# Four-entry projections: the second token tile unit by unit, and a ninth buffer for split weights

## The chip, the cores and the metric

The kernel runs on one core of a Trainium2 chip. The metric is the device time of one execution in microseconds; of several runs the median is taken. Durations inside an execution come from one profiled run, which records every instruction of the five engines: TensorE (PE, matmuls), VectorE (DVE), ScalarE (ACT), GpSimd (POOL) and SyncE (SP, which issues the loads).

## The reference

A transformer of two blocks on 256 tokens of 1024 features, in fp32. What matters here, cut down:

```python
def first_block(x, p, ...):
    h = h + 0.5 * _swiglu(_rmsnorm(h, ffn1_norm), ffn1_w_in, ffn1_w_out)      # f1
    z = _rmsnorm(h, mix_norm) @ w_in                                          # mi
    h = h + concatenate([_conv_module(...), _gla(...)]) @ w_out               # mo
    h = h + 0.5 * _swiglu(_rmsnorm(h, ffn2_norm), ffn2_w_in, ffn2_w_out)      # f2
    gate = sigmoid(_rmsnorm(h, ple_norm) @ ple_w_gate)                        # pg
    h = h + gate * (p @ ple_w_proj)                                           # pp
    return _rmsnorm(h, final_norm)

def second_block(x, c, ...):
    for i in range(2):
        mod = silu(c) @ ada_w[i] + ada_b[i]                                   # ada
        x = x + 0.5 * g1 * swiglu(modulate(rms_norm(x, ...), sh1, sc1), ...)  # f3, f5
        h = modulate(rms_norm(x, ...), sh2, sc2)
        mix = diff_attention(h, ...) if i == 0 else spatial_gating(h, ...)    # qkv, wo; si, so
        x = x + g2 * mix
        x = x + 0.5 * g3 * swiglu(modulate(rms_norm(x, ...), sh3, sc3), ...)  # f4, f6
        x = rms_norm(x, ln_out[i])
    return x
```

The comments are the names that the kernel gives to the weights of each stage. The SwiGLU's inner width is 2816.

## The kernel before, in words

**Tokens and weights.** The 256 tokens are two tiles of 128 (`NT`). All weights come from HBM as a stream of 317 tiles of 1 MB, in the order in which the stages use them; the tile with number i is called `raw`i while it is loaded. `N_RAW = 3` tiles are in flight or in use at a time, so a load is issued when the tile three before it is done with. A tile is two units of 128 x 1024.

**Split weights.** To keep fp32 accuracy, each unit is split in a high half `wh`, an ACT cast (L208), and a low half `wl`, a DVE subtraction (L209). Activations are split in the same way (`xh` and `xl`, `g`, `yHL`, `cHL`, `oHL`; L513 and L514). Every product is three matmuls: high by high, high by low, low by high (L505 to L507, and L707 where the weights are stationary). `N_HL = 8` is the number of units that may be live as pairs `wh`, `wl`; `wh14_0` is the high half of unit 0 of tile 14. Tiles of kind `ada` are not split: DVE multiplies them by `cact` and accumulates (L462).

**What sets the order.** `Stream.pump` walks the stream and issues the next cast and subtraction as soon as fewer than `N_HL` units are live. `get` hands a unit to a matmul; `release` says that its last matmul has been issued, and pumps. The program is written once, in Python, and each instruction is given a priority; every engine then runs its instructions in the order that results. So the number of live units and the place of a release decide where a cast stands among ACT's other work.

**The FFNs.** An FFN works in 11 chunks of 256 inner columns (`NCH`). From the third chunk on, `chunkT` computes gate and up of a chunk for both token tiles at once (L707, tile `gu`, two banks of 128 columns each); `evac` takes SiLU of the gate on ACT (`s`, L749), multiplies by up on DVE (`g`, L751), and splits `g`. The down products go to `acc`, four banks of 128 x 512 (two token tiles by two column halves), and are issued between the gate/up matmuls of later chunks. The banks of `gu` are used in turn: the next chunk's first matmul needs the `g` that last read its bank. In f1, ACT also makes scaled identity matrices for the convolution (`diag`, L853).

**The four-entry projections.** `pg`, `wo` and `so` (1024 x 1024) are four weight tiles, eight units, worked by `down2`: token tile 0, first four units; token tile 1, units 0 and 1; tile 0, last four units, after which `fin(0)` adds tile 0 to the residual `h0` and starts its norm; then token tile 1, the six units left, first column half and then second; `fin(1)`. `down` releases a unit in the second column half. The norm that follows is, for each tile t, a sum of squares on ACT (`ss`), `nv`t on DVE (L533), an rsqrt on POOL (`rn`, L519), `xn` on DVE and ACT (L575, L577), a transpose on PE (`xT`, L586), the modulation `xa` on DVE and ACT (L595, L599), and the split `xh`, `xl` (L513, L514).

Of the kernel before, what the change touches and what calls it, by code (L numbers as in the profile page):

```python
# [21 lines left out]
NT = S // P  # L22
# [8 lines left out]


N_RAW = 3
N_HL = 8
BUFS = {
    "row": (4, 4), "b4": (6, 4),
    "c0": (3, 2), "c1": (3, 2), "g2": (8, 2), "m": (6, 2), "ev": (4, 1),
# [118 lines left out]
def w_at(key):  # L156

    stationary = (key[0].endswith("_gu") and key[1] >= HEAD) or key[:2] in (("mi", 1), ("mi", 2))
    return W_AT if stationary else 0


class Stream:
# [23 lines left out]
    def pump(self, now=False, n=0):  # L186
# [4 lines left out]
        while 2 * self.n_split + self.half < end and (now or not k.held):  # L191
# [3 lines left out]
            if key[0] == "ada":  # L195
# [3 lines left out]
                continue  # L199
            if len(self.live) >= N_HL:  # L200
                return
            u = self.half
            raw = self.raw[i]
            at = slice(w_at(key), w_at(key) + 1024)
            h = k.wpool.tile([P, 1024 + W_PAD], F32R, tag="wh", name=f"wh{i}_{u}", bufs=N_HL)[:, at]
            l = k.wpool.tile([P, 1024 + W_PAD], F32R, tag="wl", name=f"wl{i}_{u}", bufs=N_HL)[:, at]
            with k.ahead(-BEHIND):
# [29 lines left out]
class Kernel:  # L237
# [423 lines left out]
    def fin(self, **kw):  # L661
        def f(t):
            self.xtask[t] = self.spawn(self.finish(t, **kw))
        return f
# [37 lines left out]
    def mmT(self, out, w, x, first, last):  # L702
# [6 lines left out]
            )  # L709
        self.tick(0.33)  # L710

    def down(self, t, units, first, last):

        for hf in range(2):
            sl = slice(hf * 512, hf * 512 + 512)
            for n, (key, u, x) in enumerate(units):
                h, l = self.ws.get(key, u)
                self.mm3(
                    self.acc[t][hf], x, (h[:, sl], l[:, sl]), first and n == 0, last and n == len(units) - 1
                )  # L720
                if t == NT - 1 and hf == 1:
                    self.ws.release(key, u)

    def down2(self, name, order, xs, fin):


        self.new_acc()

        def units(t, g, lo=0, hi=4):
            x = xs(t, g)  # L730
            e = order[2 * g : 2 * g + 2]
            return [((name, e[n // 2]), n % 2, x[n]) for n in range(lo, hi)]

        self.down(0, units(0, 0), True, False)
        self.down(1, units(1, 0, 0, 2), True, False)
        self.down(0, units(0, 1), False, True)
        fin(0)
        self.down(1, units(1, 0, 2, 4) + units(1, 1), False, True)
        fin(1)

    def ffn(self, name, fin):
# [944 lines left out]
```

## Time and profile before

| | |
|---|---|
| median of three runs | 1484.52 us |
| the three runs | 1482.23, 1484.52, 1487.17 us |
| the profiled run | 1483.39 us |
| its span, first to last instruction | 1481.6 us |
| PE / DVE / ACT busy | 98% / 73% / 53% of the span |
| granted TensorE clock, mean | 0.999 |
| HBM read | 343.47 MB, 233 GB/s over the span |
| 16 DMA engines busy, main queue | 62.8% |

The span of the profiled run is 1.8 us short of its time, and the profiled run is 1.1 us short of the median. "Busy" is the time in which an engine had an instruction under way. Matmuls are pipelined, so a matmul's own duration is longer than the time from its start to the start of the next; where PE's pace matters, the starts are read. A note such as [0.36 <-DVE xn] behind a row says that the engine was idle for 0.36 us before it and that the DVE instruction that wrote `xn` ended the wait.

### The profile page before, as it was taken

Reading aid. Unit: us, or ns where it says so; the run is one execution under the profiler, and the core shown is the slowest. Engines: PE = TensorE matmul, PEld = TensorE weight load, DVE = VectorE, ACT = ScalarE, POOL = GpSimd, SP = SyncE. Lnnn points to the kernel's source line nnn. Section 1 sums busy time; section 2 is a strip of 40 time slices with the busy share of each in tenths; the row PEclk is TensorE's granted clock in tenths of the full one; section 3 lists DMA queues with packets and bytes.
Section 4 is the critical chain, followed back from the end, with each engine's and each line's share of the span. In section 5 each row is a group of like instructions: output and inputs, shape, how many; then the busy total and the mean of one; then the engine's idle time right before and its main releaser. Section 6 shows DMA issues by size and latency. Waiting matters only on the chain.

```text
span 1481.6 us, 23272 instructions
## 1 busy us (share of the span) xinstructions
PE 1456.1 (98%) x9256; PEld 1299.3 (88%) x9256; DVE 1084.9 (73%) x1694; ACT 781.1 (53%) x1238; POOL 51.2 (3%) x59
## 2 busy tenths in 40 slices
PE   8999999999999999999999999999999999999997
PEld 6999989779999878999777899998899988899997
DVE  6876569978765687875688888866887668685554
ACT  6554566265444684444587544446544455554442
POOL 1000000100000000000021100000000000000000
PEclk9999999999999999999999999999999999999999
DMA  8887545138776448786345389963898846376550
GB/s 320 337 309 272 188 150 182 67 127 319 302 274 247 160 148 318 303 322 230 141 162 198 142 330 347 345 228 125 324 341 347 289 150 229 111 289 226 207 206 29
DMA packets 52333, 346.06 MB, mean 234 GB/s; under 512 B 5913, under 2 KB 8705, under 8 KB 11777
## 3 DMA queue, kind: packets, MB, share of 16 engines
q1 hardware_dynamic: 52224, 344.58, 62.8%
q8 instruction: 72, 1.18, 0.3%
q14 instruction: 37, 0.30, 0.1%
HBM read 343.47 MB, written 1.09 MB: 233 GB/s over the span
## 4 chain that ended last, share of the span: by engine, by line
PE 82%; DVE 9%; ACT 3%; issue 2%; DMA 2%; POOL 2%; SPq 0%; POOLq 0%; DVEq 0%; ACTq 0%
PE gu L707 40%; PE acc L506 9%; PE acc L507 9%; PE acc L505 9%; DVE wl L209 4%; PE gu L506 2%; PE gu L505 2%; PE gu L507 2%; DMA raw<-wpack 2%; PE xT L586 1%; ACT wh L208 1%; DVE cacc L839 1%; POOL rn L519 1%; PE cv L863 1%; PE qkv L505 0%
## 5 line engine op out<-in xcount | busy, mean ns | idle before, releaser
L209 DVE TENSOR_TENSOR wl<-raw,wh 128x1024 fp32r<-128x1024 f32 x490 | 588.4, 1221 | 242.4 <-ACT wh L208 240.2
L208 ACT CAST wh<-raw 128x1024 fp32r<-128x1024 f32 x490 | 502.4, 1051 | 397.3 <-DMA raw<-wpack 166.9
L707 PE MATMUL gu<-xh,wh 128*128 128x256 f32 x1728 | 484.3, 280 | 1.2 <-DVE g L751 0.8
L707 PE MATMUL gu<-xl,wh 128*128 128x256 f32 x1728 | 482.5, 279 | 0.0
L707 PE MATMUL gu<-xh,wl 128*128 128x256 f32 x1728 | 482.0, 279 | 0.0
L707 PEld LDWEIGHTS gu<-xh,wh 128*128 128x128 f32 x1728 | 324.8, 188 | 4.6 <-DVE g L751 1.4
L707 PEld LDWEIGHTS gu<-xl,wh 128*128 128x128 f32 x1728 | 324.8, 188 | 2.5
L707 PEld LDWEIGHTS gu<-xh,wl 128*128 128x128 f32 x1728 | 324.8, 188 | 0.0
L506 PE MATMUL acc<-wh,g 128*128 128x512 f32 x528 | 206.7, 391 | 0.0
L507 PE MATMUL acc<-wl,g 128*128 128x512 f32 x528 | 206.1, 390 | 0.0
L505 PE MATMUL acc<-wh,g 128*128 128x512 f32 x528 | 205.7, 391 | 0.0
L462 DVE SCALAR_TENSOR_TENSOR raw<-raw,cact 128x1024 f32<-128x1024 f32 x144 | 171.7, 1218 | 16.4 <-DMA raw<-wpack 16.3
L507 PEld LDWEIGHTS acc<-wl,g 128*128 128x128 f32 x528 | 99.1, 188 | 21.0
L506 PEld LDWEIGHTS acc<-wh,g 128*128 128x128 f32 x528 | 99.1, 188 | 19.8 <-DVE g L514 1.4
L505 PEld LDWEIGHTS acc<-wh,g 128*128 128x128 f32 x528 | 99.1, 188 | 19.2
L749 ACT ACTIVATE s<-gu 128x256 f32<-128x256 f32 x108 | 40.8, 385 | 76.2 <-PE gu L707 76.0
L505 PE MATMUL gu<-wh,xh 128*128 128x512 f32 x192 | 75.7, 395 | 2.0 <-ACT wh L208 1.6
L507 PE MATMUL gu<-wl,xh 128*128 128x512 f32 x192 | 75.1, 393 | 1.5 <-DVE wl L209 1.5
L506 PE MATMUL gu<-wh,xl 128*128 128x512 f32 x192 | 75.2, 393 | 0.5 <-DVE xl L514 0.5
L751 DVE TENSOR_TENSOR g<-gu,s 128x256 f32<-128x256 f32 x108 | 44.5, 420 | 28.2 <-ACT s L749 28.1
L513 ACT CAST g<-g 128x256 fp32r<-128x256 f32 x108 | 43.1, 405 | 39.1 <-DVE g L751 38.4
L519 POOL TENSOR_TENSOR rn<-nv,neghalf 128x1 f32<-128x1 f32 (+1 forms) x22 | 20.1, 913 | 1238.1 <-DVE nv L533 1020.6
(308 smaller groups left out, 1611.3 us busy)
## 6 DMA issues: line engine op xcount, KB each, us to landing
raw<-wpack SPq DMA_DIRECT2D x316, 1024.0 KB, 5.0
gate<-grow SPq DMA_DIRECT2D x6, 512.0 KB, 4.6
row<-rows SPq DMA_DIRECT2D x5, 512.0 KB, 5.7
bias<-fd SPq DMA_DIRECT2D x16, 128.0 KB, 3.9
raw<-wpack SPq DMA_DIRECT2D x2, 512.0 KB, 6.7
out<-h SPq DMA_DIRECT2D x4, 256.0 KB, 2.2
h<-x SPq DMA_DIRECT2D x2, 256.0 KB
h<-x SPq DMA_DIRECT2D x1, 512.0 KB
```

The source lines that it names most:

```text
L208: self.last = k.after(nc.scalar.copy(out=h, in_=raw[:, u, :]))
L209: self.last_l = k.after(nc.vector.tensor_sub(out=l, in0=raw[:, u, :], in1=h.bitcast(F32)))
L462: self.after(nc.vector.scalar_tensor_tensor(out=raw[:, u, :], in0=raw[:, u, :], scalar=1.0, in1=self.cact, op0=ALU.mult, op1=ALU.mult, acc ...
L505: nc.tensor.matmul(out, lhsT=xh, rhs=wh, start=first, stop=False)
L506: nc.tensor.matmul(out, lhsT=xl, rhs=wh, start=False, stop=False)
L507: nc.tensor.matmul(out, lhsT=xh, rhs=wl, start=False, stop=last)
L513: self.nc.scalar.copy(out=dst[0], in_=src),
L519: self.nc.gpsimd.tensor_tensor(out=r, in0=v, in1=self.neghalf[:, :n], op=ALU.pow)
L586: self.last_T = nc.tensor.transpose(ps[:, i, :], xn[hf][:, i * P : (i + 1) * P], self.ident)
L707: nc.tensor.matmul(out, lhsT=ww, rhs=xx, start=first and n == 0, stop=last and n == 2, skip_group_check=True)
L749: nc.scalar.activation(s, b[:, 0, :], AF.Silu)
L751: nc.vector.tensor_mul(out=y, in0=b[:, 1, :], in1=s)
```

## The change

`N_HL` goes from 8 to 9. In `down2` the last call for token tile 1 is taken apart: the two units that are left of the first four go through the new `down_by_unit`, which does both column halves of a unit and releases it at once; the last four units go through `down` as before.

```diff
-N_HL = 8
+N_HL = 9
...
+    def down_by_unit(self, units):
+
+
+        for key, u, x in units:
+            h, l = self.ws.get(key, u)
+            for hf in range(2):
+                sl = slice(hf * 512, hf * 512 + 512)
+                self.mm3(self.acc[NT - 1][hf], x, (h[:, sl], l[:, sl]), False, False)
+            self.ws.release(key, u)
+
...
         fin(0)
-        self.down(1, units(1, 0, 2, 4) + units(1, 1), False, True)
+        self.down_by_unit(units(1, 0, 2, 4))
+        self.down(1, units(1, 1), False, True)
         fin(1)
```

Behind the new function the lines of the file are 10 or 11 higher: SiLU in an FFN is L749 before and L760 after, the SwiGLU product L751 and L762, the convolution's `diag` L853 and L864.

How the order of the engines' instructions moves is shown at three places. The names carry the tile's name and a running number; the rows stand in program order.

**First place: ACT and DVE in f1, third chunk.** ACT before, from the cast of weights 12 on; `s_75` and `s_78` are the SiLUs of the third chunk's two banks `gu_51` and `gu_52`:

```order
L208 CAST wh12_0_524<-raw12_402 128x1024
L208 CAST wh12_1_573<-raw12_402 128x1024
L853 ACTIVATE diag_72_560<-kc_80,cols_81 128x128
L749 ACTIVATE s_75_583<-gu_51_416 128x256
L749 ACTIVATE s_78_588<-gu_52_417 128x256
L513 CAST g_77_587<-g_76_585 128x256
L208 CAST wh14_0_619<-raw14_498 128x1024
L513 CAST wglr_64_542<-wg_63_540 128x8x16
L513 CAST g_80_592<-g_79_590 128x256
L208 CAST wh14_1_626<-raw14_498 128x1024
L208 CAST wh15_0_658<-raw15_577 128x1024
```

ACT after, from the same cast:

```order
L208 CAST wh12_0_500<-raw12_396 128x1024
L208 CAST wh12_1_528<-raw12_396 128x1024
L208 CAST wh14_0_583<-raw14_474 128x1024
L864 ACTIVATE diag_73_570<-kc_80,cols_81 128x128
L208 CAST wh14_1_623<-raw14_474 128x1024
L208 CAST wh15_0_632<-raw15_532 128x1024
L208 CAST wh15_1_662<-raw15_532 128x1024
L760 ACTIVATE s_75_587<-gu_51_420 128x256
L864 ACTIVATE diag_73_570<-kc_80,cols_81 128x128
L760 ACTIVATE s_78_592<-gu_52_421 128x256
```

The two SiLUs stood ahead of all four casts of weights 14 and 15; now the first stands behind the four, and the second behind one more `diag`. DVE in the same place, before, from the last subtraction of weights 12; `g_76` and `g_79` are the SwiGLU products made from `s_75` and `s_78`:

```order
L209 TENSOR_TENSOR wl12_1_574<-raw12_402,wh12_1_573 128x1024
L462 SCALAR_TENSOR_TENSOR raw13_406,ada_31_252<-raw13_406,cact_88 128x1024 x2
L751 TENSOR_TENSOR g_76_585<-gu_51_416,s_75_583 128x256
L478 TENSOR_TENSOR mod_86_713<-ada_31_252,cols_81 128x8
L751 TENSOR_TENSOR g_79_590<-gu_52_417,s_78_588 128x256
L481 SCALAR_TENSOR_TENSOR mod_86_713<-mod_86_713,cols_81 128x8
L514 TENSOR_TENSOR g_77_587<-g_76_585,g_77_587 128x256
L209 TENSOR_TENSOR wl14_0_620<-raw14_498,wh14_0_619 128x1024
```

DVE after:

```order
L209 TENSOR_TENSOR wl12_1_529<-raw12_396,wh12_1_528 128x1024
L462 SCALAR_TENSOR_TENSOR raw13_400,ada_31_252<-raw13_400,cact_88 128x1024 x2
L478 TENSOR_TENSOR mod_86_689<-ada_31_252,cols_81 128x8
L481 SCALAR_TENSOR_TENSOR mod_86_689<-mod_86_689,cols_81 128x8
L209 TENSOR_TENSOR wl14_0_584<-raw14_474,wh14_0_583 128x1024
L209 TENSOR_TENSOR wl14_1_624<-raw14_474,wh14_1_623 128x1024
L209 TENSOR_TENSOR wl15_0_633<-raw15_532,wh15_0_632 128x1024
L209 TENSOR_TENSOR wl15_1_663<-raw15_532,wh15_1_662 128x1024
L762 TENSOR_TENSOR g_76_589<-gu_51_420,s_75_587 128x256
L462 SCALAR_TENSOR_TENSOR raw16_536,ada_84_668<-raw16_536,cact_88 128x1024
```

The product `g_76` stood right behind the `ada` step on tile 13, ahead of the subtractions of weights 14; now it stands behind those of weights 14 and 15, and `g_79` behind the first step on the `ada` tile 16.

**Second place: PE in f1, where the gate/up matmuls of the next chunk begin.** They write the bank `gu_82` and use weights 9; `acc_47` to `acc_50` are the four banks of the down product. Before:

```order
L507 MATMUL acc_47_412<-wl12_1_574,g_61_451 128x512
L505 MATMUL acc_48_413<-wh12_0_524,g_59_445 128x512
L506 MATMUL acc_48_413<-wh12_0_524,g_59_445 128x512
L507 MATMUL acc_48_413<-wl12_0_525,g_59_445 128x512
L707 MATMUL gu_82_632<-xh_86,wh9_0_388 128x256
L707 MATMUL gu_82_632<-xl_87,wh9_0_388 128x256
L707 MATMUL gu_82_632<-xh_86,wl9_0_389 128x256
L707 MATMUL gu_82_632<-xh_86,wh9_0_388 128x256
```

After:

```order
L506 MATMUL acc_50_419<-wh12_0_500,g_59_449 128x512
L507 MATMUL acc_50_419<-wl12_0_501,g_59_449 128x512
L505 MATMUL acc_50_419<-wh12_1_528,g_61_455 128x512
L506 MATMUL acc_50_419<-wh12_1_528,g_61_455 128x512
L507 MATMUL acc_50_419<-wl12_1_529,g_61_455 128x512
L707 MATMUL gu_82_636<-xh_86,wh9_0_382 128x256
L707 MATMUL gu_82_636<-xl_87,wh9_0_382 128x256
L707 MATMUL gu_82_636<-xh_86,wl9_0_383 128x256
L707 MATMUL gu_82_636<-xh_86,wh9_0_382 128x256
```

Before, nine down matmuls of weights 12 stand ahead of the first gate/up matmul and the other fifteen behind the chunk; now all twenty-four stand ahead, up to the last on `acc_50`.

**Third place: DVE at the start of f4, the norm of token tile 1 after `wo`.** `gy` and `h1` are the residual's second column half, `nv1` and `xn` the norm. Before:

```order
L552 TENSOR_TENSOR gy_1075_8572<-acc_1019_8315,gate_686_6464 128x512
L209 TENSOR_TENSOR wl171_0_8516<-raw171_8287,wh171_0_8515 128x1024
L554 TENSOR_TENSOR h1_79<-gy_1075_8572,h1_79 128x512
L209 TENSOR_TENSOR wl171_1_8520<-raw171_8287,wh171_1_8519 128x1024
L533 SCALAR_TENSOR_TENSOR nv1_1078_8580<-ss1_1068_8556 128x1
L209 TENSOR_TENSOR wl172_0_8526<-raw172_8309,wh172_0_8525 128x1024
L575 TENSOR_SCALAR xn_1081_8590<-h1_79,rn1_1079_8582 128x512
L209 TENSOR_TENSOR wl172_1_8530<-raw172_8309,wh172_1_8529 128x1024
```

After, to the same `xn`:

```order
L209 TENSOR_TENSOR wl171_1_8520<-raw171_8281,wh171_1_8519 128x1024
L552 TENSOR_TENSOR gy_1075_8576<-acc_1019_8319,gate_686_6462 128x512
L209 TENSOR_TENSOR wl172_0_8526<-raw172_8303,wh172_0_8525 128x1024
L554 TENSOR_TENSOR h1_79<-gy_1075_8576,h1_79 128x512
L209 TENSOR_TENSOR wl172_1_8530<-raw172_8303,wh172_1_8529 128x1024
L209 TENSOR_TENSOR wl173_0_8536<-raw173_8413,wh173_0_8535 128x1024
L533 SCALAR_TENSOR_TENSOR nv1_1078_8584<-ss1_1068_8560 128x1
L209 TENSOR_TENSOR wl173_1_8543<-raw173_8413,wh173_1_8542 128x1024
L575 TENSOR_SCALAR xn_1081_8594<-h1_79,rn1_1079_8586 128x512
```

Two subtractions of weights 171 stood ahead of `nv1` and one of 172 ahead of `xn`; now the first unit of 171 is far ahead, and the subtractions go up to `wl173_0` ahead of `nv1` and to `wl173_1` ahead of `xn`. The same shift, with its own numbers, stands in the program at the start of f6, and on DVE at the start of f3 (`wl112_0` instead of `wl111_0` ahead of `xn` of tile 1).

## Rows read from the trace of the kernel before

**Rows 1.** Page, part 1: engine, busy us (share of the span), instructions
```profile
PE 1456.1 (98%) x9256; PEld 1299.3 (88%) x9256; DVE 1084.9 (73%) x1694; ACT 781.1 (53%) x1238; POOL 51.2 (3%) x59
```

**Rows 2.** Waits of PE: instruction and what ended it, us in total, times, longest
```profile
PE xT L586 <- DVE xn L575: 4.6, 11, 0.7
...
PE gu L507 <- DVE wl L209: 1.5, 2, 1.0
...
PE qT L1247 <- DVE qn L1243: 1.3, 1, 1.3
...
PE acc L505 <- ACT cHL L513: 1.1, 1, 1.1
...
PE gu L707 <- DVE g L751: 0.8, 1, 0.8
...
PE gu L707 <- DVE g L790: 0.4, 1, 0.4
```

**Rows 3.** Page, part 5: busy us, mean ns | idle before, releaser
```profile
L209 DVE TENSOR_TENSOR wl<-raw,wh 128x1024 fp32r<-128x1024 f32 x490 | 588.4, 1221 | 242.4 <-ACT wh L208 240.2
...
L208 ACT CAST wh<-raw 128x1024 fp32r<-128x1024 f32 x490 | 502.4, 1051 | 397.3 <-DMA raw<-wpack 166.9
```

**Rows 4.** Timeline of ACT, f1: start us, us, [idle before]
```profile
49.89 2.00 ACT L208 CAST wh<-raw 128x1024 fp32r<-128x1024 f32 x2 [1.70 <-DMA raw<-wpack]
...
52.10 0.64 ACT L749 ACTIVATE s<-gu 128x256 f32<-128x256 f32 x2
...
56.31 1.05 ACT L208 CAST wh<-raw 128x1024 fp32r<-128x1024 f32 x1
```

**Rows 5.** Timeline of DVE, same stretch
```profile
55.54 0.42 DVE L751 TENSOR_TENSOR g<-gu,s 128x256 f32<-128x256 f32 x1
...
56.07 0.42 DVE L751 TENSOR_TENSOR g<-gu,s 128x256 f32<-128x256 f32 x1
```

**Rows 6.** Timeline of PE, same stretch
```profile
55.46 0.39 PE L506 MATMUL acc<-wh,g 128*128 128x512 f32 x1
55.69 0.39 PE L507 MATMUL acc<-wl,g 128*128 128x512 f32 x1
56.02 0.39 PE L707 MATMUL gu<-xh,wh 128*128 128x256 f32 x1
56.24 0.28 PE L707 MATMUL gu<-xl,wh 128*128 128x256 f32 x1
56.36 0.28 PE L707 MATMUL gu<-xh,wl 128*128 128x256 f32 x1
```

**Rows 7.** DMA issues from 53.3 to 53.5: KB each, us to landing
```profile
raw<-wpack SPq DMA_DIRECT2D x1, 1024.0 KB, 5.2
```

**Rows 8.** Timeline of PE, end of the mixer
```profile
304.87 0.50 PE L505 MATMUL acc<-wh,cHL 128*128 128x512 f32 x1 [1.08 <-ACT cHL L513]
```

**Rows 9.** Timeline of DVE, end of the mixer
```profile
304.85 0.69 DVE L514 TENSOR_TENSOR cHL<-cs,cHL 128x512 fp32r<-128x512 f32 x1 [0.22 <-ACT cHL L513]
```

**Rows 10.** Timeline of DVE, start of f3
```profile
542.23 0.49 DVE L575 TENSOR_SCALAR xn<-h,rn 128x512 f32<-128x512 f32 x1 [0.59 <-POOL rn L519]
```

**Rows 11.** Timeline of DVE, attention
```profile
802.96 0.17 DVE L1295 RECIPROCAL rs<-sm 128x4 f32<-128x4 f32 x1
```

**Rows 12.** Timeline of PE, attention
```profile
810.01 0.66 PE L1311 MATMUL aT<-kc,s 128*128 128x128 f32 x4 [0.32 <-DVE on L1348]
```

**Rows 13.** Timeline of DVE, start of f4
```profile
846.14 0.48 DVE L575 TENSOR_SCALAR xn<-h,rn 128x512 f32<-128x512 f32 x1 [0.45 <-POOL rn L519]
```

**Rows 14.** Timeline of PE, start of f4
```profile
846.69 0.65 PE L586 MATMUL xT<-kc,xn 128*128 128x128 f32 x4 [0.36 <-DVE xn L575]
```

**Rows 15.** Timeline of DVE, start of f6
```profile
1294.15 0.49 DVE L575 TENSOR_SCALAR xn<-h,rn 128x512 f32<-128x512 f32 x1 [0.44 <-POOL rn L519]
```

**Rows 16.** Timeline of PE, warming matmuls at the start
```profile
1.50 4.64 PE L436 MATMUL warm<-one,ones_r 128*128 128x512 f32 x10 [1.50 <-POOL one L431]
...
7.73 2.11 PE L436 MATMUL warm<-one,ones_r 128*128 128x512 f32 x8
```

## The prediction

> **What bounds the kernel now.** The page's first part comes first: TensorE (PE) is busy for 1456.1 us of a span of 1481.6, 98% [rows 1]. So the time is PE's matmuls plus the places where PE stands still, and a change that leaves the matmuls alone can only add to or take from the still places. The list of PE's waits says how much there is to take: the largest single kinds are 4.6 us for `xn`, 1.5 for a low half `wl` of the weights, 1.1 for `cHL` and 0.8 for a SwiGLU product `g` [rows 2]. Nothing that a ninth weight buffer could fill is larger than those 1.5 us. Then the page's costliest groups: a unit of weights costs ACT one cast of 1.05 us and DVE one subtraction of 1.22 us, 490 times each [rows 3]. These two are the coins in which this change pays, because in the trace ACT and DVE start their instructions in the order of the program, and the change moves casts and subtractions ahead of other work.
>
> **What the change does.** It adds and removes no matmul, cast, subtraction or load; each engine has as many rows as before. In the four-entry projections the second token tile's first units are freed earlier, and one more unit may be in flight, so nearly every cast and subtraction moves one unit forward. Where the engine in question has only casts around it, that costs nothing. It costs where something that PE waits for stands right behind.
>
> **Step 1, the third chunk of f1.** Before, ACT casts chunk weights 12, then runs SiLU `s_75`, `s_78` at 52.10 and only then casts `wh14_0` at 56.31 [rows 4]. DVE makes the two `g` at 55.54 and 56.07, 0.42 each [rows 5]. PE leaves the `acc` matmuls of weights 12 after the one at 55.69 and starts the next gate/up matmul at 56.02, as soon as the first `g` has freed its PSUM bank: a hole of 0.1 us [rows 6]. After, `s_75` stands behind four more casts, the last two of weights 15; `g` stands behind `wl15_1`; and PE runs 15 more `acc` matmuls before it comes to the gate/up matmul (the order rows show all three).
>
> Fifteen matmuls at the 0.23 us from one start to the next [rows 6] end the cover at 55.92 + 3.45 = 59.37. The load of weights 15 can't start sooner than before: it takes the buffer that `wl12_1` frees, and it was issued at 53.36 and took 5.2 us [rows 7], so it lands at 58.55. Two casts then end at 60.6, `s_75` at 60.9; the two subtractions behind the casts end near 61.95 (the second can't start before 60.6, and the first fills 59.6 to 60.8), and `g_76` at 62.35. PE is idle from 59.37 to 62.4: **3.05 us**. The gate/up matmuls of the chunk's second 128 columns stand seven behind (0.12 us apart [rows 6], so 63.2) and need `g_79`, behind one `ada` multiply-add over a tile of a subtraction's size (1.2, [rows 3]) and a small subtraction (0.1): 62.35 + 1.3 + 0.42 = 64.05, another **0.85**. With 0.2 for the fourth chunk, which is shuffled too but has 17 matmuls of its first 128 columns to run before it needs the second `g`, step 1 is **+4.1**. Low bound 2.6 (load half a microsecond faster, second `g` covered half); high bound 5.8 (fourth chunk not covered: a cast and a `g` more).
>
> **Step 2, end of the mixer.** PE stands 1.08 us for `cHL` before 304.87 [rows 8]. After, ACT has two casts of weights 60 ahead of the activations that make it, where it had the two of weights 59; DVE has three subtractions left before the low half of `cHL` where it had two, which moves that from 304.85 [rows 9] by one, 1.15 less the 0.22 it was idle. **+0.9**, bounds 0 and 1.2.
>
> **Step 3, gate projection to f3.** Here the change helps first: `wl110_0` is made well before the norm, so the longest wait for `wl`, 1.0 us [rows 2], goes. But tile 1's norm chain on DVE gets three subtractions ahead of it instead of one and a `g` inside it, which moves `xn` from 542.23 [rows 10] by about 4 us. PE has tile 0's matmuls of weights 112 moved ahead to cover most; by my row-by-row reckoning tile 1 starts 1.4 us later on balance, and PE reaches the two later waits for `g`, 0.8 and 0.4 us [rows 2], with these done. **0**, bounds -2.7 (the three waits go, 1.0 + 0.8 + 0.4 and the 0.2 or so that a restart costs each; tile 1 hidden) and +1.5.
>
> **Step 4, attention.** `wl168_0` now stands ahead of the softmax reciprocal of 802.96 [rows 11]; its cast waits for two units of ACT work, so the reciprocal moves to about 806.8. Of these 3.9 us PE covers most with value matmuls that it now does first; it already waited 0.32 at the transposes of 810.01 [rows 12], so anything uncovered shows. Between 0, all covered, and 3.9, nothing covered, I choose a third, **+1.2**, since there are value matmuls for the greater part but the transposes wait already.
>
> **Step 5, attention output to f4, gating output to f6.** DVE had `wl171_1` before `nv1`, `wl172_0` before `xn` of tile 1 (846.14 [rows 13]); after, it has `wl172_1`, `wl173_0` before `nv1` and `wl173_1` before `xn` as well. `h1` now ends near 844.1 and is followed by 2.3 us of subtractions, `nv1` at 846.5, another subtraction, `xn` at 847.9 to 848.4: about 1.8 us late. PE waited for it 0.36 us before 846.69 already [rows 14]. Tile 0's matmuls on weights 172 and 173, which come ready sooner, fill 0.9 of this; the low half `xl` behind one more subtraction adds 0.4. **+1.3** each. The gating output has the same rows at 1294.15 [rows 15]: together **+2.6**, bounds 0 and 5.2. Other stage borders (f1 to mixer, f4 to f5) shift by the same one unit on every engine: 0.
>
> **Sum.** 4.1 + 0.9 + 0 + 1.2 + 2.6 = **+8.8 us**. The profiled execution took 1483.39 us (span 1481.6); that makes 1492.2. The median of the runs shown is 1.1 above the profiled one, so a median is forecast at **1493**. The low bounds add to -0.1, the high ones to +17.6.
>
> **A page against the row.** The trace's longest hole in PE inside the kernel is some 1.3 us [rows 2], and the granted clock is 0.999 of 2.4 GHz over the span; a hole of 3.05 us is beyond what it shows. At the start, ten warming matmuls took 4.64 us and eight later ones 2.11, so 0.46 against 0.26 each [rows 16]. If such a slow stretch came after the hole in step 1, it would cost 4.64 - 10 x 0.26 = 2.0 us more. The Trainium skill, "TensorE: Matmul & The Clock Gate", section "Why this matters for your kernels", warns that idle gaps between bursts of matmuls send the array back to half clock; no row here shows it, and by that rule the sum would be 10.8 instead of 8.8. The Trainium skill, "Perfetto Trace Analysis", section "Optimization Strategy", says that the same gap repeating on the engine that should be saturated can mean too few buffers; by it the ninth buffer would gain. PE's waits for `wl` are two in the whole span [rows 2], so the repeating gap isn't there.
>
> **Rivals.**
> *The ninth buffer pays.* The waits of step 3 go (-2.7), and the fillers that the new order moves ahead cover what steps 2, 4 and 5 delay. This needs step 1 to be no loss: the load of weights 15 would have to land by 55.5, 2.1 us after its issue, so that `g` is done by 59.3. The one load took 5.2 us [rows 7]; against. Time 1484.5 - 2.7 = 1481.8, and 1479.5 if half of the 4.6 us that PE waits for `xn` [rows 2] went with it. Chance 0.15.
> *Only f1 loses.* Step 1 stands, step 3 gains its 2.7, and half of steps 2, 4 and 5 is covered (2.35): 4.1 - 2.7 + 2.35 = +3.75, 1488.3, which can't be told from no change. For it: PE has fillers moved ahead at each of these places. Against: PE already waited at each. Chance 0.22, from 1482 to 1488.9.
> *The slow stretch.* Forecast plus 2.0: 1495. Chance 0.06.
> *The forecast*, chance 0.57.
>
> **How the numbers follow.** A measurement of this kernel tells 0.3%, 4.5 us, from no change: faster is under 1480.0, slower over 1489.0. The first rival's two times lie on either side of the lower bound, so its chance is halved between them. Slower: 0.57 + 0.06 = 0.63. Same: 0.22 + 0.08 = 0.30. Faster: 0.07. The range leaves out the faster half of the first rival and the top of the summed bounds, about one in ten at each end: 1481 to 1499; the forecast's own range is 1489 to 1498.
>
> **What would show it.** In the trace after: a hole of about 3 us in PE between 59 and 63, ended by the SiLU product, with `s` starting after the second cast of weights 15; a second hole of nearly 1 us right behind; no wait for `wl` near 537; `xn` of tile 1 about 4 us later near 546, and 1.8 later (after subtracting what PE has lost so far) near 848 and 1296; the reciprocal 4 us later in the attention. The prediction is wrong if PE has no hole near 60, which would say that ACT or the load had more slack than the rows show; or if the holes are there and the time isn't, which would say that PE makes idle time up later, where in this trace there is hardly any to make up.

## The result, and the profile after

The changed kernel takes 1495.15 us in the median (1494.33 to 1495.58, four runs), the kernel before 1483.74 (1482.23 to 1487.17, four runs): a ratio of 1.0073 with a 95% interval of 1.0061 to 1.0085, 0.7% slower. Its profiled run took 1495.58 us, with a span of 1493.4, against 1481.6 before. PE has as many matmuls as before, 9256, and all of the loss lies in the places where it stands still or runs slowly.

Where in the kernel the time goes is read from the first transposes (`xT`) of each stage's norm, which are the same instructions in both traces:

| first `xT` after | before, us | after, us | difference | in this part |
|---|---|---|---|---|
| start | 6.88 | 7.30 | +0.42 | +0.42 |
| f1 | 194.49 | 200.14 | +5.65 | +5.23 |
| mixer | 314.80 | 323.96 | +9.16 | +3.51 |
| f2, gate projection, f3 | 720.61 | 727.72 | +7.11 | -2.05 |
| attention | 835.73 | 845.18 | +9.45 | +2.34 |
| attention output, f4 | 1022.62 | 1033.09 | +10.47 | +1.02 |
| f5 and gating unit | 1283.74 | 1294.42 | +10.68 | +0.21 |
| gating output, f6 (last matmul) | 1473.71 | 1485.57 | +11.85 | +1.17 |

The waits of PE after, in the form of [rows 2] (instruction and what ended the wait, us in total, times, longest):

```profile
PE xT L586 <- DVE xn L575: 4.8, 11, 1.2
PE gu L707 <- DVE g L762: 3.3, 2, 2.7
PE qT L1258 <- DVE qn L1254: 2.0, 2, 1.4
PE gu L506 <- DVE xl L514: 1.9, 4, 0.7
...
PE acc L505 <- ACT cHL L513: 1.4, 1, 1.4
PE gu L507 <- DVE wl L209: 0.8, 2, 0.5
PE acc L506 <- DVE cHL L514: 0.7, 1, 0.7
```

The `g` of L751 is L762 here. Its 3.3 us in two waits are new and lie in f1; the one wait of 0.8 that it had before, in f3, is gone, and so is the wait of 0.4 for the other `g`. `cHL` has grown from 1.1 to 1.4 and its low half has a wait of its own, 0.7; a second wait for `qn` is new; the long wait for `wl` is down from 1.0 to 0.5. The waits for `xl` add up to 1.9 in four; before there was one, in the mixer:

```profile
PE gu L506 <- DVE xl L514: 0.5, 1, 0.5
```

The first hole, in the timeline of PE in f1, where [rows 6] showed 0.1 us:

```profile
59.49 0.39 PE L507 MATMUL acc<-wl,g 128*128 128x512 f32 x1
62.55 0.39 PE L707 MATMUL gu<-xh,wh 128*128 128x256 f32 x1 [2.66 <-DVE g L762]
...
63.36 0.28 PE L707 MATMUL gu<-xh,wh 128*128 128x256 f32 x1
64.32 0.55 PE L707 MATMUL gu<-xh,wh 128*128 128x256 f32 x1 [0.68 <-DVE g L762]
64.67 0.42 PE L707 MATMUL gu<-xl,wh 128*128 128x256 f32 x1
64.89 0.42 PE L707 MATMUL gu<-xh,wl 128*128 128x256 f32 x1
...
67.42 0.28 PE L707 MATMUL gu<-xh,wh 128*128 128x256 f32 x1
67.53 0.28 PE L707 MATMUL gu<-xl,wh 128*128 128x256 f32 x1
```

PE ends the down product with the matmul at 59.49 and starts gate and up at 62.55, 2.83 us after its next slot at 59.72. Behind seven of these matmuls it stands again for 0.68 us. The timeline of ACT shows why; the two casts are those of weights 15, and `s` comes right behind:

```profile
58.72 2.00 ACT L208 CAST wh<-raw 128x1024 fp32r<-128x1024 f32 x2 [0.94 <-DMA raw<-wpack]
60.62 0.38 ACT L760 ACTIVATE s<-gu 128x256 f32<-128x256 f32 x1
```

and the timeline of DVE, the two subtractions of weights 15 and the two products:

```profile
59.80 2.36 DVE L209 TENSOR_TENSOR wl<-raw,wh 128x1024 fp32r<-128x1024 f32 x2 [0.77 <-ACT wh L208]
62.08 0.42 DVE L762 TENSOR_TENSOR g<-gu,s 128x256 f32<-128x256 f32 x1
...
63.76 0.42 DVE L762 TENSOR_TENSOR g<-gu,s 128x256 f32<-128x256 f32 x1
```

The second surprise stands in the PE rows above: behind the holes the matmuls start 0.22 us apart (64.67 to 64.89) where they start 0.11 us apart at 67.42 to 67.53. The windows view gives for each stretch the busy time of PE, PEld (TensorE's weight loads), DVE, ACT and POOL, then the granted clock (PEclk), the share of the DMA engines and their GB/s. The first three rows belong to f1, the last one to the mixer:

```profile
59.30:62.50 3.20, 0.58 (x3) 0.16 (x1) 2.70 (x4) 2.55 (x6) 0.00 (x0) 1.00 0.96 389
...
64.30:67.40 3.10, 3.08 (x14) 3.10 (x15) 2.82 (x5) 1.27 (x2) 0.00 (x0) 0.51 0.99 314
67.40:75.00 7.60, 7.60 (x67) 7.60 (x66) 4.49 (x5) 3.75 (x5) 0.00 (x0) 1.00 0.69 260
312.00:316.00 4.00, 3.28 (x9) 2.26 (x9) 2.96 (x4) 2.19 (x5) 0.00 (x0) 0.64 0.94 385
```

The clock is 0.51 of full speed from 64.3 to 67.4, the lower of its two levels (1.2 against 2.4 GHz), and 1.00 again from 67.4 on. What PE did before it fell: 0.58 us of matmuls in 3.2 us. At the mixer's end PE stands for `cHL`, 1.42 us where [rows 8] had 1.08, and again for its low half, which it didn't before:

```profile
311.73 0.73 PE L505 MATMUL acc<-wh,cHL 128*128 128x512 f32 x2 [1.42 <-ACT cHL L513]
313.18 0.79 PE L506 MATMUL acc<-wh,cHL 128*128 128x512 f32 x1 [0.72 <-DVE cHL L514]
...
314.20 0.63 PE L505 MATMUL acc<-wh,cHL 128*128 128x512 f32 x1
314.63 0.63 PE L506 MATMUL acc<-wh,cHL 128*128 128x512 f32 x1
```

Behind this, matmuls of 512 columns start 0.43 us apart (314.20 to 314.63), nearly twice the 0.23 of [rows 6]. Another wait of 0.5 us in the mixer, for `ke`, is new as well. The low half of `cHL` is late because three subtractions run ahead of it on DVE:

```profile
309.04 3.49 DVE L209 TENSOR_TENSOR wl<-raw,wh 128x1024 fp32r<-128x1024 f32 x3
312.44 0.69 DVE L514 TENSOR_TENSOR cHL<-cs,cHL 128x512 fp32r<-128x512 f32 x1
```

### The profile page after: what moved, and what is told of

Same layout as the page of the kernel before. It is cut to its first block, busy times and chain, and to the rows that moved or that the text cites. A ratio compares the mean times of both kernels' runs of the same rounds, so it can differ in the third digit from the quotient of the medians.

```text
span 1493.4 us, 23243 instructions
## 1 busy us (share of the span) xinstructions
PE 1462.2 (98%) x9256; PEld 1301.7 (87%) x9256; DVE 1087.1 (73%) x1694; ACT 782.2 (52%) x1238; POOL 50.8 (3%) x59
## 4 chain that ended last, share of the span: by engine, by line
PE 81%; DVE 10%; ACT 3%; issue 3%; DMA 2%; POOL 1%; SPq 0%; POOLq 0%; ACTq 0%; DVEq 0%
PE gu L707 40%; PE acc L506 9%; PE acc L507 9%; PE acc L505 9%; DVE wl L209 4%; PE gu L506 2%; PE gu L507 2%; PE gu L505 2%; DMA raw<-wpack 1%; ACT wh L208 1%; PE xT L586 1%; POOL rn L519 1%; PE qk L707 1%; DVE cacc L850 1%; ACT s L1302 1%
## 5 line engine op out<-in xcount | busy, mean ns | idle before, releaser
L760 ACT ACTIVATE s<-gu 128x256 f32<-128x256 f32 x108 | 40.6, 383 | 85.0 <-PE gu L707 84.9
L762 DVE TENSOR_TENSOR g<-gu,s 128x256 f32<-128x256 f32 x108 | 44.6, 421 | 34.2 <-ACT s L760 34.1
```

The lines of the kernel that those rows point to most:

```text
L760: nc.scalar.activation(s, b[:, 0, :], AF.Silu)
L762: nc.vector.tensor_mul(out=y, in0=b[:, 1, :], in1=s)
```

## The experiments

Each kernel was compared with the kernel before, run on the same chip. Theory A is that of the prediction: the ninth buffer moves casts and subtractions ahead of work that PE waits for. Theory B is its rival: the early release in the projections makes the loss. Where parts are named, they are those of the table above, read in the same way from each kernel's trace.

**One half of the change at a time.** First the ninth buffer alone:

```diff
 # kernel before
-N_HL = 8
+N_HL = 9
```

> Nine buffers, the projections as before (half by half). The order of ACT and DVE equals that of the changed kernel everywhere but around the three projections. Theory A (the ninth buffer makes the loss: it moves casts ahead of what PE waits for in f1, at the mixer's end and in the attention): f1 +5.2, mixer +3.5, attention +2.3 stay, so 1483.7 + 11.0 = 1494.7 us, 1493 to 1496. Theory B (the early release in the projections makes it): 1483.7 to 1486 us.

It took 1494.57 us, a ratio of 1.0078 (1.0065 to 1.0091), inside the expected range. That the total was hit so closely is partly luck: in its trace f1 costs 8.45 us and the mixer 1.35, where 5.2 and 3.5 had been expected, f2 to f3 gain 2.25, the attention costs 2.13, and f5 has a wait of 1.5 us for `gc` that neither of the other two kernels has. Up to the gate projection this kernel and the changed one run the same instructions in the same order, so 5.2 and 8.45 in f1, and 3.5 and 1.35 in the mixer, are values of two executions and no property of the one or the other kernel.

Then the new function alone:

```diff
 # changed kernel
-N_HL = 9
+N_HL = 8
```

> Eight buffers, the projections unit by unit. f1 and the mixer then have the order of the kernel before. Theory A: only the three projections can differ, -1.8 at the gate projection and +1.0 and +1.2 at the other two: 1483 to 1485 us, no hole in PE near 60. Theory B: nearly all of the loss, 1492 us or more.

It took 1482.59 us, a ratio of 0.9997 (0.9988 to 1.0006), a little under the expected range: the gain at the gate projection is 1.0 and not 1.8, and the losses expected at the other two projections are 0.0. The timeline of PE with the new function alone shows the end of the down product and the first gate/up matmul in f1 as before:

```profile
55.95 0.39 PE L507 MATMUL acc<-wl,g 128*128 128x512 f32 x1
56.24 0.38 PE L707 MATMUL gu<-xh,wh 128*128 128x256 f32 x1
```

Theory B is out. The loss belongs to the ninth buffer. The trace of the kernel with the buffer alone also shows the clock, in two windows, f1 behind the hole and the mixer behind its two waits:

```profile
64.50:69.00 4.50, 3.74 (x17) 3.77 (x18) 3.35 (x9) 1.45 (x2) 0.00 (x0) 0.50 0.90 335
...
313.50:317.50 4.00, 3.25 (x13) 2.39 (x14) 3.25 (x4) 2.50 (x5) 0.00 (x0) 1.00 0.93 381
```

and the timeline of PE in its mixer:

```profile
313.54 0.73 PE L505 MATMUL acc<-wh,cHL 128*128 128x512 f32 x2 [1.42 <-ACT cHL L513]
314.98 0.50 PE L506 MATMUL acc<-wh,cHL 128*128 128x512 f32 x1 [0.71 <-DVE cHL L514]
```

In f1 the clock fell here too, behind a longer hole (3.8 us), and 28 matmuls ran at the slow pace and not 14. In the mixer it did not fall, though PE waited 1.42 and 0.71 us, as long as in the changed kernel, where it fell to 0.64. The traces of eight kernels in this study have these two waits, 1.4 and 0.7 us; in two of them (the changed kernel and the one with the filled hole below) the clock fell behind them, in six it stayed at 1.00. So these waits let the clock fall in some executions and not in others.

**f1 by itself.** At most eight units live until f1 ends:

```diff
-            if len(self.live) >= N_HL:
+            if len(self.live) >= self.limit:
...
+        self.ws.limit = 8
         self.ffn("f1", ...)
+        self.ws.limit = 9
         self.mixer(...)
```

> The changed kernel, but at most eight units live until f1 ends, nine from the mixer on. Theory A: the two holes and the slow stretch of f1 go, 5.2 us, and nothing else: 1495.2 - 5.2 = 1490.0 us, 1489 to 1491. Rival (idle time early in the kernel is made up later, since PE waits less for weights afterwards): over 1493 us. The mixer's holes should stay at the size they have in the changed kernel, 3.5 us in all.

It took 1488.46 us, 1.0035 (1.0021 to 1.0049): 6.7 less than the changed kernel, more than the 5.2 expected, and the idle time isn't made up later. In its trace f1 costs nothing (-0.2), so all of the 5.2 came back there. Its mixer cost 1.7 us (the first `xT` behind it at +1.39, after -0.32), not 3.5: the waits were 1.4 and 0.7 as in the changed kernel, without the slow stretch. Against that, the attention output with f4 cost 2.5 and not 1.0.

Then the hole was closed without a buffer less, by an order constraint alone:

```diff
-                nc.scalar.activation(s, b[:, 0, :], AF.Silu)
+                i = nc.scalar.activation(s, b[:, 0, :], AF.Silu)
...
-                nc.vector.tensor_mul(out=y, in0=b[:, 1, :], in1=s)
+                m = nc.vector.tensor_mul(out=y, in0=b[:, 1, :], in1=s)
+                if name == "f1" and j == HEAD:
+                    self.pin(i)
+                    self.pin(m)
```

> The changed kernel, nine units all through, but in the third chunk of f1 the SiLUs and the products of the SwiGLU are held ahead of the next casts and subtractions (an order constraint on ACT and DVE, no buffer less). If the place of the casts makes the hole, and not the number of buffers or the load: no hole near 60, the 5.2 us of f1 go, 1495.2 - 5.2 = 1490.0 us, 1489 to 1491. If the loads or the ninth buffer itself make it, over 1493 us.

It took 1490.12 us, 1.0044 (1.0032 to 1.0057), inside the expected range. On ACT both SiLUs now run before the casts of weights 15:

```profile
57.61 0.64 ACT L760 ACTIVATE s<-gu 128x256 f32<-128x256 f32 x2
...
59.88 1.05 ACT L208 CAST wh<-raw 128x1024 fp32r<-128x1024 f32 x1
```

and PE goes from the down product to gate and up without a hole:

```profile
60.38 0.40 PE L507 MATMUL acc<-wl,g 128*128 128x512 f32 x1
60.62 0.28 PE L707 MATMUL gu<-xh,wh 128*128 128x256 f32 x1
```

So the place of the casts makes the hole; nine buffers by themselves don't. The time agrees for another reason than the expected one, though: f1 still costs 2.4 us in this trace, with a wait of 1.0 us for `g` in the fourth chunk, near 74, so 2.9 of its 5.2 came back and not all. The mixer gave the rest: 1.4 and not 3.5, since the clock didn't fall there. Two kernels below have the same constraint and the same nine buffers, and f1 costs 0.3 and 1.4 in their traces.

**The clock.** Twelve matmuls whose result nobody reads were put in the hole of f1 (the chunk's second 128 columns then also begin behind fifteen matmuls of the first 128 and no longer behind seven); `first` is the first gate/up matmul of the chunk:

```diff
+            first = self.mms[at]
...
+            if name == "f1" and j == 3:
+                ps, i = self.pst("warm"), self.mms[-1]
+                for _ in range(12):
+                    i = self.after(nc.tensor.matmul(
+                        ps, lhsT=self.ones_r, rhs=self.xh[:, 0, 0:4, :], start=True, stop=True
+                    ), i)
+                self.after(first, i)
```

> The changed kernel with twelve matmuls of 128x512 into a spare PSUM tile, which nobody reads, between the last down matmul of weights 12 and the gate/up matmul behind the hole in f1: 12 x 0.23 = 2.7 us of a hole of 3.05. They feed nothing, so the SiLU product is ready when it was. Theory C (the hole lets TensorE's clock fall, and the matmuls behind it run at 0.21 us instead of 0.12): the granted clock stays 1.00 there and 1.3 us come back, 0.7 more where the second hole is covered by matmuls that now stand ahead of it: 1493.2 us, 1492.6 to 1494.2. Rival D (the matmuls behind the hole are slow for another reason, such as the waiting ACT and DVE work or the loads running then): spacing stays 0.21 for some 14 matmuls, 1494.4 to 1495.2 us.

It took 1494.05 us in the median, 1.0071 (1.0059 to 1.0084), and its five times lie between 1489.8 and 1495.3; the median alone doesn't separate the theories. The trace, of an execution of 1493.04 us, does. The windows of the stretches shown above:

```profile
59.30:62.50 3.20, 3.20 (x16) 2.44 (x15) 3.19 (x4) 2.48 (x6) 0.00 (x0) 1.00 1.02 397
...
64.30:67.40 3.10, 3.10 (x29) 3.10 (x28) 3.10 (x5) 2.34 (x3) 0.00 (x0) 1.00 0.73 272
```

and the timeline of PE:

```profile
59.24 2.88 PE L821 MATMUL warm<-xh,ones_r 128*128 128x512 f32 x12
62.06 0.39 PE L709 MATMUL gu<-xh,wh 128*128 128x256 f32 x1
62.28 0.28 PE L709 MATMUL gu<-xl,wh 128*128 128x256 f32 x1
```

With PE busy through the hole the clock stays at 1.00 and the matmuls start 0.12 us apart from the second on. DVE and ACT are no less busy beside them than in the changed kernel (3.10 and 2.34 us in the second window, against 2.82 and 1.27), and the DMA engines are as busy in the first window and less so in the second (0.73 against 0.99). So rival D is out as far as it means ACT and DVE, and with the clock read at 0.51 in the one trace and 1.00 in the other it is the clock. In this trace f1 costs 3.4 us (+2.90 after -0.53) against 5.2.

**What the sizes add up to.** With at most eight units until the mixer ends, nine from f2 on:

```diff
         self.mixer(...)
+        self.ws.limit = 9
         self.ple_load()
```

> The changed kernel with at most eight live units until the mixer ends, nine from f2 on. Theory A with the sizes read so far: f1 and mixer as before, -1.8 at the gate projection, +2.1 in the attention, +2.2 at the starts of f4 and f6, 0.2 elsewhere: +2.7 on 1483.3, 1486.0 us, 1485 to 1487. Rival (the gain at the gate projection and the losses behind it depend on what came before): outside 1485 to 1487.

It took 1489.07 us, 1.0044 (1.0032 to 1.0057): outside. Its trace, of the fastest of its five executions (1487.05), has the mixer's two waits, 1.4 and 0.7 us, and costs 2.0 there although eight units were live; the other parts are as expected within 0.3. The next kernel shows why. With nine only from f2 to the gate projection, and the new function at the gate projection alone:

```diff
+        self.ws.limit = 8
         self.ffn("f3", ...)
...
+        if name == "pg":
+            self.down_by_unit(units(1, 0, 2, 4))
+            self.down(1, units(1, 1), False, True)
+        else:
+            self.down(1, units(1, 0, 2, 4) + units(1, 1), False, True)
```

> Nine live units only from f2 to the gate projection, the early release only in the gate projection, everything else with eight units and half by half. Theory A: only the gain of the gate projection is left, -1.8: 1481.5 us, 1481 to 1482.3, a ratio of 0.9988, and no hole beyond those of the kernel before. Rival (the gain is lent: f3 catches up and the time ends where it was): 1483 to 1484 us.

It took 1485.63 us, 1.0018 (1.0009 to 1.0027): 4.1 more than expected. The gain from f2 to f3 is there, -2.2, but it is lost elsewhere. The waits of PE in it:

```profile
PE acc L506 <- ACT cHL L514: 1.4, 1, 1.4
PE aT L1326 <- DVE on L1363: 1.4, 1, 1.4
...
PE acc L507 <- DVE cHL L515: 0.7, 1, 0.7
```

The mixer has both waits of the changed kernel (+2.25 in that part), and the attention one of 1.4 us for `on` where the kernel before had 0.3 (+1.2). The limit counts live units; the ninth buffer was still there, and with it the casts were free to move. The expectation had taken a limit for a buffer. For the mixer this was tested, by an order constraint that holds the casts and subtractions of weights 60 in place; for the attention it was not:

```diff
+            if i == 60:
+                k.after(self.last, k.c_end[0])
+                k.after(self.last_l, k.c_end[1])
```

> As the kernel with nine units only from f2 to the gate projection and the early release there alone (1485.6 us, 4 more than expected), but the casts and subtractions of weights 60 are held behind the first cHL at the mixer's end, where the trace of that kernel still had them ahead of it: its ninth buffer let the casts move although eight units were live. If their place makes the mixer's loss, its hole before cHL is back at 1.1 us or less, the mixer costs 2.0 us less: 1483.6 us, 1482.6 to 1484.4. If the loss has another cause: 1485 to 1486 us.

It took 1484.19 us, 1.0007 (0.9999 to 1.0016). One wait for `cHL` is left, and the low half's is gone:

```profile
PE acc L509 <- ACT cHL L517: 1.3, 1, 1.3
```

The part costs 0.9 us and not 2.25. With this constraint the mixer costs 0.5 to 0.9 us in three traces (this one and the last two below), without it 1.35 to 2.25 in the six in which the clock didn't fall there. So the place of the casts makes the greater part of the mixer's loss too. The wait for `cHL` was expected back at 1.1 or less and is 1.3; what makes the 0.9 that are left wasn't looked into. The new function in all three projections, in the kernel with nine units from f2 to the gate projection:

```diff
-        if name == "pg":
-            self.down_by_unit(units(1, 0, 2, 4))
-            self.down(1, units(1, 1), False, True)
-        else:
-            self.down(1, units(1, 0, 2, 4) + units(1, 1), False, True)
+        self.down_by_unit(units(1, 0, 2, 4))
+        self.down(1, units(1, 1), False, True)
```

> As the kernel with nine units only from f2 to the gate projection, but with the early release in all three projections; the attention output and the gating output then have it with eight units. Theory A (a loss at f4 and f6 needs both the early release and the ninth unit): within 0.5 us of that kernel, 1481.5 us. Rival (the early release alone costs there): +2.2, 1483.7 us.

It took 1487.49 us, 1.0025 (1.0016 to 1.0034), with eleven times from 1484.1 to 1489.7, 6 us more than theory A and 3.8 more than the rival. The profiled execution is the fastest and shows none of the extra time; in it the parts with f4 and f6 cost 0.1 and 0.3, so the early release costs little there as long as eight units are live. Then six matmuls that nobody reads were put in its mixer hole:

```diff
+        ps, i = self.psg("warm"), self.mms[-1]
+        for _ in range(6):
+            i = self.after(self.nc.tensor.matmul(
+                ps, lhsT=self.ones_r, rhs=self.yg[1][0].rearrange("p a b -> p (a b)"), start=True, stop=True
+            ), i)
...
+            if t == 0:
+                self.after(self.mms[at], i)
+                self.after(self.mms[at + 1], i)
```

> As the kernel with nine units only from f2 to the gate projection and the early release in all three projections, whose eleven times lie between 1484.1 and 1489.7 us, with six matmuls of 128x512 that nobody reads in the hole before cHL (6 x 0.23 = 1.4 us of 1.44). If the spread comes from TensorE's clock, which falls behind this hole in some executions and not in others: all times within 2.5 us of each other, median 1484 to 1485.5. If it comes from elsewhere: median near 1487.5 and the same spread.

It took 1486.10 us, 1.0023 (1.0014 to 1.0032), from 1484.5 to 1489.4, ten of the eleven within 2.2 us. The range of the ten is narrower, the median is not where the clock theory put it, and one execution is as long as before: inconclusive.

**Nine buffers and two constraints.** Both order constraints in the changed kernel, the one on the SiLUs and products of f1 and this:

```diff
+            if i == 60:
+                k.after(self.last, k.c_end[0])
+                k.after(self.last_l, k.c_end[1])
```

> The changed kernel, nine units all through, with the SiLUs of f1's third chunk ahead of the casts (1490.1 us without the following) and the casts and subtractions of weights 60 behind the first cHL. Place of the casts as the cause: the mixer's part of the loss goes too, 1.4 us of holes and now and then a slow stretch: 1488.4 us, 1487.4 to 1489.2; what is left over the kernel before, 5 us, lies in the attention, f4, f6 and the rest of f1. Rival: 1490 us.

It took 1488.87 us, 1.0042 (1.0030 to 1.0053), from 1486.4 to 1492.3, as expected in the median. And with the new function at the gate projection alone:

```diff
-        self.down_by_unit(units(1, 0, 2, 4))
-        self.down(1, units(1, 1), False, True)
+        if name == "pg":
+            self.down_by_unit(units(1, 0, 2, 4))
+            self.down(1, units(1, 1), False, True)
+        else:
+            self.down(1, units(1, 0, 2, 4) + units(1, 1), False, True)
```

> As the kernel with nine units all through, the SiLUs of f1 and the convolution's cHL held ahead of the casts (1488.9 us, from 1486.4 to 1492.3), but with the early release at the gate projection alone. If the loss at the starts of f4 and f6 needs the ninth unit and the early release together, 2.2 us go and so do the two waits for xl there: 1486.7 us, 1485.5 to 1487.7. If the ninth unit alone makes it: 1488.9 us with the waits as they were.

It took 1485.13 us, 1.0011 (1.0002 to 1.0020), from 1484.2 to 1485.8, below the expected range. The waits for `xl` in the first of the two:

```profile
PE gu L509 <- DVE xl L517: 1.8, 4, 0.6
```

and in the second:

```profile
PE gu L509 <- DVE xl L517: 0.6, 2, 0.3
```

In the traces the parts with f4 and f6 go from 1.1 each to 0.1 and 0.0, the 2.2 us that were expected. So the loss at f4 and f6 needs the ninth unit and the early release together: with the buffer alone, and with the function alone, these two parts came out within 0.1 us of before as well.

In the medians 3.7 us went and not 2.2, and the spread shrank from 5.9 us to 1.7. Of the eight kernels here with nine buffers and the early release at `wo` and `so`, six have executions 3 to 6 us above their fastest (the changed kernel's own four lie within 1.3, those with eight units in f1 within 1.8); of the five that lack one of the two none goes beyond 2.9. The kernel before has one of 1487.17, 4.9 above the fastest of its four. That points to the pair but doesn't show it. Three traces say what a part of it is: in the kernels with eight units in f1, with the filled hole and with the SiLUs held, none of them the fastest of its executions, the part with f4 costs 2.0 to 2.5 us, and not 1.0 to 1.1 as in the other traces with nine units there. In the first of the three, PE waits for a SwiGLU product in f4:

```profile
902.42 0.39 PE L708 MATMUL gu<-xh,wh 128*128 128x256 f32 x1 [0.84 <-DVE g L763]
```

and on ACT the two casts ahead of its SiLU start, when their load has landed, 2.9 us later (the first row) than in the kernel with eight units to the mixer's end (the second), which reaches f4 at the same time and doesn't wait there for `g`:

```profile
897.12 2.00 ACT L209 CAST wh<-raw 128x1024 fp32r<-128x1024 f32 x2 [6.62 <-DMA raw<-wpack]
894.25 2.01 ACT L209 CAST wh<-raw 128x1024 fp32r<-128x1024 f32 x2 [5.99 <-DMA raw<-wpack]
```

So in this trace a load that lands late holds up the SiLU behind its casts, as in f1.

No version beats the kernel before by more than its interval; the best two, the function alone and the kernel with nine units from f2 to the gate projection and the casts held at the mixer's end, can't be told from it.

## Why the prediction was right, by its own steps

The forecast was 1493, the time 1495.15, inside its own range of 1489 to 1498. Measured by the table above, its sum of +8.8 came out at 11.4 between the first `xT` and the last matmul. The mechanism, casts and subtractions ahead of what PE waits for, is the one that the experiments show. That the total came so close is partly luck: the slow matmuls, some 2.9 us, were not in the sum, and the gain of 2.05 in step 3, put at 0, pays for most of them. And the sizes of steps 1 and 2 change from one execution to the next, as the kernel with the buffer alone shows (8.45 and 1.35 us).

**Step 1**, +4.1, measured 5.2. The mechanism held in every part: `s` behind the second cast of weights 15 (60.62, forecast 60.6), `g` at 62.08 (61.95), a hole of 2.83 us (3.05) and a second one of 0.84 over the usual pace (0.85). The fourth chunk cost nothing here. What is missing is the slow stretch: 14 matmuls at 0.21 us and not 0.12, 1.3 us. It was given as a rival at 2.0 us and a chance of 0.06, on the ground that no row showed a hole so long. The Trainium skill's "TensorE: Matmul & The Clock Gate", section "Why this matters for your kernels", warned of it; the trace agrees, 0.51 behind the hole and 1.00 when the hole is filled.

**Step 2**, +0.9, measured 3.5; the largest error of size. The waits for `cHL` grew by 0.3 and 0.7 us, 1.0 in all, close to what was worked out; the slow stretch behind them, some eight matmuls at 0.43 and not 0.23 (1.6 us), wasn't in the term, since I tied the rival to step 1 alone, and neither was the new wait of 0.5 us for `ke`. In the six traces with both waits in which the clock didn't fall there, the part cost between 1.35 (buffer alone) and 2.25 us.

**Step 3**, 0, measured -2.05. The gain stood where it was put: the long wait for `wl` is gone, and so are both later waits for `g`. But `xn` came late by less:

```profile
553.73 0.48 DVE L575 TENSOR_SCALAR xn<-h,rn 128x512 f32<-128x512 f32 x1 [0.81 <-POOL rn L519]
```

less the 8.8 us that PE had lost at the gate projection's first `xT` it is 544.9, 2.7 after the 542.23 of [rows 10], not 4, and what tile 1 loses is made up within f3, where the two waits for `g` were. The measured value lies near the low bound. Both halves of the change gain here by themselves: -2.25 with the buffer alone, -1.0 with the function alone.

**Step 4**, +1.2, measured 2.3. The reciprocal stands behind the subtraction, as said:

```profile
812.66 0.17 DVE L1306 RECIPROCAL rs<-sm 128x4 f32<-128x4 f32 x1
```

Less the 7.1 us lost before, that is 805.55, 2.6 late and not 3.9. The loss is larger all the same. PE also waits for `qn` a second time (0.6 us of the 2.0 above), which the step left out; but its waits in the whole part add up to 2.9 us before and 3.3 after, so the waits don't account for the greater share of the 2.3. No experiment held this part's order in place: that the reciprocal's place makes the loss is argued and not shown.

**Step 5**, +2.6, measured 1.0 and 1.2. `xn` is late by as much as said (the timeline of DVE; less 9.45 it is 848.15, 2.0 after [rows 13]):

```profile
857.60 0.49 DVE L575 TENSOR_SCALAR xn<-h,rn 128x512 f32<-128x512 f32 x1 [0.45 <-POOL rn L519]
```

but PE's matmuls on tile 0 cover it: the wait before the transposes is 0.33 us, 0.36 in [rows 14]. The loss comes where the step had put the smaller share, at `xl`:

```profile
858.14 1.09 PE L586 MATMUL xT<-kc,xn 128*128 128x128 f32 x8 [0.33 <-DVE xn L575]
...
863.77 0.50 PE L506 MATMUL gu<-wh,xl 128*128 128x512 f32 x1 [0.64 <-DVE xl L514]
```

**The rivals.** That the ninth buffer pays is out, by the kernel with the buffer alone. That only f1 loses is out, by the mixer and the attention in the changed kernel's trace. The slow stretch was no rival to the forecast but a part of what happened, twice, and its time, 1495, is the one that was measured.

**What stays open.** What the executions 3 to 6 us above the fastest spend is seen only in part, in f4 in the three traces above, and why a load lands late there is not known. The clock can explain a part of the rest, where the mean granted clock of an execution is 0.997 and the mixer's waits may have let it fall. It doesn't explain all: the slowest execution with the early release in all three projections (1489.73 us) and the slowest with the mixer's hole filled (1489.43) have 0.999, as much as the kernel before. The attention's loss was not taken apart by an experiment.

## What to carry to other kernels

A buffer more is no free gain where, as here, ACT and DVE run their instructions in program order: it lets preparation move ahead, also ahead of the evacuation that the bound engine waits for, so read the order of the changed program at every place where that engine has a narrow cover, and price the queue ahead of the late instruction. If such a wait on PE grows by microseconds, add the slow matmuls behind it. If the deeper prefetch is wanted, hold the urgent instructions ahead of it by an order constraint; here that took back 2.9 to 4.9 us of f1's 5.2, in three traces, and 1.3 in the mixer. And read the parts of a total that was hit: twice here the time came out as expected from other parts than the expected ones.

## What the runs showed of the hardware that was not expected

TensorE's clock fell to its lower level behind a pause inside a busy kernel: 0.51 over 3.1 us after 0.58 us of matmuls in 3.2, with 256-column matmuls 0.21 us apart; twelve idle-filling matmuls kept it at 1.00. Two shorter waits, 1.42 and 0.7 us with 0.7 us of matmuls between them, were followed by a mean of 0.64 over 4 us in the changed kernel's trace, by 0.66 over 5 us in that of the kernel with the filled hole, and by 1.00 in six others, with waits of the same length. The mean granted clock of an execution hardly shows such falls: the changed kernel's trace, with two of them, has 0.997, the kernel before 0.999.
